# Eight head pairs and the attention gates as seven block products, made behind the first values

## The chip, the cores and the metric

One core of a Trainium2 chip runs the whole layer in one launch. The metric is the time of one execution in device microseconds, taken as the median of several runs. TensorE (PE) multiplies, VectorE (DVE) and ScalarE (ACT) compute on tiles of 128 partitions, GpSimd (POOL) helps, and SyncE (SP) issues most DMAs.

## The reference, cut to what matters

The layer takes 1024 tokens of width 1024. One input projection gives queries, keys and values of 24 heads of width 64, a Fourier input of width 512, and two sigmoid gates of width 1024. The heads stand in three groups of eight, with dilations 1, 4 and 16.

```
proj = x @ w_in                      # 1024 x 7168
q, k, v = 24 heads of 64 each;  u_f = 512 columns
gate_a, gate_f = sigmoid(two slices of 1024 columns)
for each group: banded attention, queries scaled by 1/8, bias by T5 bucket
attn   = softmax over groups of the log-sums, applied to the three outputs
merged = gate_a * (attn @ w_attn_out) + gate_f * (fourier(u_f) @ w_fourier_out)
h = layer_norm(ALPHA * x + merged @ w_out)
h = layer_norm(ALPHA * h + squared_relu_mlp(h))
```

## The kernel before

All large products are split in two float32r parts, high and low: `split` (L62) rounds on ACT (L63) and takes the rest on DVE (L64), and `mm3` (L73) issues three matmuls (L75 to L77) for each pair of 128 x 128 weights and 128 x 512 data.

The activations come transposed, as eight tiles of 128 channels x 1024 tokens. The kernel loads and splits one after the other and keeps the parts `xh`, `xl` in the ring `U` (31 slots of 4 KB a partition) until the last gate is made. While they come in, the values of group 0 are accumulated over the eight tiles in all eight PSUM banks (L113 to L141). Other rings are `wr` (3 raw weights), `w` (10 split weights), `S` (8 half tiles) and `PT` (6 half tiles).

Twelve head pairs follow (L368 to L379). Before each `attention` the pair's queries and keys are made by `project` (L182): two blocks of 128 columns, each of two halves of tokens and eight contraction tiles, so 96 matmuls, straight into `U` tiles in SBUF. Groups 1 and 2 turn the token order as they copy out of PSUM (L194 to L203). `values` (L143) makes all eight value tiles of the next group at once, behind the second pair of a group. `attention` (L222) works in units: scores on PE (L237), bias and running minimum on DVE (L245), exponent on ACT (L248), transposes on PE (L262), copies on DVE and ACT (L270 to L276), products with the values (L291), copies out (L303). At its end ACT issues the small DMAs of the row sums (L322 to L328; four to a pair in groups 0 and 2, sixteen in group 1).

The Fourier branch comes next. In its last loop (L546) each of eight column blocks makes its gate from `xh`, `xl` (`gates`, L338, 48 matmuls) and `combine` (L421) joins the three groups' outputs of one head pair from DRAM, behind blocks 1, 3, 5 and behind the loop. Then the attention output runs over eight column blocks: `gates("wga", d)`, 48 matmuls, and `attn_out` (L583), 24 matmuls, with the gate applied on DVE (L590, L591).

The up-projection of the MLP (L782) already makes pairs of column blocks as seven products of half-sized blocks in place of eight, by Strassen and Winograd's scheme: `weight_blocks` (L711) forms sums of weight blocks (L733 to L739) and splits them, `token_blocks` (L676) sums of token blocks, and each product takes 12 matmuls into a PSUM bank that later products add to.

The instructions of each engine are put in order by a scheduler when the kernel is built: among those whose inputs are ready by its cost model, the one that stands earlier in the program goes first. On the chip each engine takes its instructions in that order and waits at the first that is not ready. Tiles of a ring are handed out as others come free.

Of the kernel before, what the change touches and what calls it, by code (L numbers as in the profile page):

```python
# [11 lines left out]
F32 = mybir.dt.float32  # L12
F32R = mybir.dt.float32r
AF = mybir.ActivationFunctionType
ALU = mybir.AluOpType
# [13 lines left out]
def tile_hybrid_layer(ctx, tc, a, out):  # L29
# [57 lines left out]
    make_identity(nc, ident)  # L87


    xh, xl = [], []  # L90

    def v_cols(g, t):
        if g == 0:
            return slice(64 + 128 * t, 192 + 128 * t)
# [4 lines left out]

    def v_lhs(g, t, k):  # L100
        if g == 0 and t == 7:
            return xeh[:, k, :], xel[:, k, :]
# [6 lines left out]
    V = {0: v_alloc()}  # L109
    xTk = a["xT"].rearrange("(k p) n -> p k n", p=128)  # L110
    accs = [ps(t) for t in BANKS]
    vw = {}
    for k in range(8):  # L113
        x = wr([128, 1024])
        xh.append(U([128, 1024], F32R, "xh"))
        xl.append(U([128, 1024], F32R, "xl"))
        if k == 0:
            w0 = tmp([128, 512]), tmp([128, 512])
            for c in range(2):
                s = slice(512 * c, 512 * c + 512)  # L120
                nc.sync.dma_start(x[:, s], a["xT"][0:128, s])
                nc.sync.dma_start(w0[c], a["wv"][0, 0, :, c])
                split(x[:, s], xh[0][:, s], xl[0][:, s])
                vw[c] = tmp([128, 512], F32R), tmp([128, 512], F32R)
                split(w0[c], *vw[c])
            xeh, xel = U([128, 8, 128], F32R, "xe"), U([128, 8, 128], F32R, "xe")
# [3 lines left out]
            split(xer, xeh, xel)  # L130
        else:
            nc.sync.dma_start(x, a["xT"][128 * k:128 * k + 128])
            split(x, xh[k], xl[k])
            if k % 2 == 0:
                w = weights(a["wv"][0, k // 2], [128, 2, 512])
                for c in range(2):
                    vw[k + c] = w[0][:, c], w[1][:, c]
        for t in range(8):
            mm3(accs[t], *v_lhs(0, t, k), *vw[k], k == 0, k == 7)
    for t in range(8):  # L140
        (nc.vector.tensor_copy if t % 2 else nc.scalar.copy)(V[0][t // 2][:, t % 2], accs[t])  # L141

    def values(g):  # L143
        V[g] = v_alloc()
        w = [weights(a["wv"][g, u], [128, 2, 512]) for u in range(4)]
        for t in range(8):
# [3 lines left out]
            (nc.vector.tensor_copy if t % 2 else nc.scalar.copy)(V[g][t // 2][:, t % 2], p)  # L150


    bd = dram.tile([24, NE], F32, name="bd")
# [16 lines left out]
    def bias_tile(g, hp):  # L170
        n = 128 if g == 2 else 256
        b = tmp([128, 2, 256], name="bias")
        for hh in range(2):
            off = bd.offset + (8 * g + 2 * hp + hh) * NE + E_OFF[g]
            nc.sync.dma_start(b[:, hh, :n], bass.AP(tensor=bd.tensor, offset=off, ap=[[1, 128], [1, n]]))
        return b


    od = dram.tile([3, 4, 128, 1024], F32, name="od")
    sd = dram.tile([3, 4, 4, 1024], F32, name="sd")  # L180

    def project(g, hp):  # L182
        qk = []
        for i in range(2):
# [183 lines left out]
    todo = [(g, hp) for g in range(3) for hp in range(4)]  # L368
    cur = project(0, 0)
    bias_rows()  # L370
    for i, (g, hp) in enumerate(todo):
        bias = bias_tile(g, hp)
        attention(g, hp, *cur, bias)
        if hp == 1 and g < 2:
            values(g + 1)
        if i + 1 < len(todo):
            cur = project(*todo[i + 1])
# [168 lines left out]
    for d in range(8):  # L546
        if d == 1:
            group_weights()
        gate = gates("wgf", d, tmp) if d else gate_f0
        if d == 3:  # L550
            w4n = fourier_weights(1)
        if d % 4 == 0:
            w4, ws = w4n
        dc = slice(128 * (d % 4), 128 * (d % 4) + 128)
        yp = []
        for c0, c1 in CC:
            p = ps("s")[:, :c1 - c0]
# [24 lines left out]

    def attn_out(d, gate):  # L583
# [127 lines left out]
    def weight_blocks(pair, which):  # L711

        (wa, *wb), _ = WR.pop(pair)
        out = WB[pair]

        def put(name, src):
            t = out[name] = wh([128, 2, 512], F32R, "wb")
            split(src, t[:, 0], t[:, 1])

        sum_ = nc.vector.tensor_tensor  # L720
        a11, a12 = wa[:, :512], wa[:, 512:]
        if which != 1:
            put("A11", a11)
            put("A12", a12)
        if which == 0:
            return
        a21, a22 = wb[0][:, :512], wb[0][:, 512:]
        if pair < WHOLE:
            put("A21", a21)
            put("A22", a22)  # L730
            return
        s3 = tmp([128, 512], name="s3")
        sum_(s3, a11, a21, op=ALU.subtract)  # L733
        sum_(a21, a21, a22, op=ALU.add)
        sum_(a11, a21, a11, op=ALU.subtract)
        put("S2", a11)
        put("S1", a21)
        put("S3", s3)
        sum_(a12, a12, a11, op=ALU.subtract)  # L739
        put("S4", a12)  # L740
        put("A22", a22)


    WHOLE, START = 2, 5
# [3 lines left out]
    for hf in range(2):  # L748
        zs = [U([128, 1024], name="z") for _ in range(4)]
        stats = []  # L750
        for c in range(2):
            s = slice(512 * c, 512 * c + 512)
            w = [weights(a["wout"][c, u], [128, 2, 512]) for u in range(4)]
            for t in range(4):
# [12 lines left out]
                else:  # L767
# [376 lines left out]
```

## Time and profile before

| what | value |
|---|---|
| median of three runs | 1634.26 us (1632.04 to 1637.53) |
| profiled execution: time, span | 1630.72 us, 1628.9 us |
| PE busy | 1586.7 us, 97% of the span |
| DVE busy | 932.5 us, 57% |
| ACT busy | 604.0 us, 37% |
| POOL busy | 268.2 us, 16% |
| first projection begins | 52.98 us |
| attention stage | about 77 to 566 us |
| attention output | about 760 to 870 us |

The profile is of one execution. A busy share says how much of the span had an instruction of the engine in flight; consecutive matmuls overlap, so the distance between their starts, not the length of one, is what each costs.

### The profile page before, as it was taken

To read this page: it belongs to the slowest core of one execution; us is meant where nothing else is said; L and a number is where in the kernel's file an instruction comes from. 1 tells how busy PE (TensorE), PEld (TensorE's weight loads), DVE (VectorE), ACT (ScalarE), POOL (GpSimd) and SP (SyncE) were. 2 spreads that over 40 slices of the span, in tenths; PEclk is the share of its full clock that TensorE was granted. 3 is DMA by queue.
4 is the path that set the end of the run, shared out by engine and by line. 5 is a ranking of instruction groups with operands and counts; after the bars stand their busy time and mean duration, and the time that the engine had idled before them with its cause. 6 is when DMAs were issued, how large, how long until landed. Compare 5 with 4: busy or idle time off the path is not lost. (4 is left out here: it accounts for less than half of the span.)

```text
span 1628.9 us, 20580 instructions
## 1 busy us (share of the span) xinstructions
PE 1586.7 (97%) x7780; PEld 1296.0 (80%) x7780; DVE 932.5 (57%) x1541; ACT 604.0 (37%) x1208; POOL 268.2 (16%) x282
## 2 busy tenths in 40 slices
PE   8999999999999999999999999999999989999997
PEld 6779877897777787888888887888888778888885
DVE  4241333313233287554335787567877997878878
ACT  4251344314334454222213346553444433334312
POOL 0000001100000030000000000043333442526414
PEclk9999999999999999999999999999999999999998
DMA  7210211102111252544114442344436754535502
GB/s 225 78 55 21 78 47 53 59 15 71 56 56 44 73 169 76 172 144 143 52 65 140 157 162 106 121 155 145 152 136 240 263 193 150 181 104 168 168 14 91
DMA packets 79117, 187.25 MB, mean 115 GB/s; under 512 B 11512, under 2 KB 15032, under 8 KB 79018
## 3 DMA queue, kind: packets, MB, share of 16 engines
q1 hardware_dynamic: 64234, 151.56, 28.7%
q0 software_dynamic: 6304, 21.07, 3.3%
q10 hardware_dynamic: 8480, 13.31, 2.2%
q8 instruction: 61, 1.00, 0.3%
q14 instruction: 38, 0.31, 0.1%
HBM read 143.05 MB, written 42.86 MB: 114 GB/s over the span
## 5 line engine op out<-in xcount | busy, mean ns | idle before, releaser
L64 DVE TENSOR_TENSOR w<-wr,w 128x1024 fp32r<-128x1024 f32 x83 | 101.4, 1224 | 288.3 <-ACT w L63 288.2
L75 PE MATMUL pmm<-xh,w 128*128 128x512 f32 x640 | 253.1, 395 | 1.0 <-ACT gate L344 1.0
L77 PE MATMUL pmm<-xh,w 128*128 128x512 f32 x640 | 253.3, 396 | 0.0
L76 PE MATMUL pmm<-xl,w 128*128 128x512 f32 x640 | 252.6, 395 | 0.0
L63 ACT CAST w<-wr 128x1024 fp32r<-128x1024 f32 x83 | 87.2, 1051 | 232.1 <-PE pmm L76 184.6
L75 PEld LDWEIGHTS pmm<-xh,w 128*128 128x128 f32 x640 | 120.2, 188 | 29.4 <-issue 1.5
L76 PEld LDWEIGHTS pmm<-xl,w 128*128 128x128 f32 x640 | 120.1, 188 | 29.1 <-issue 1.2
L77 PEld LDWEIGHTS pmm<-xh,w 128*128 128x128 f32 x640 | 120.1, 188 | 28.1 <-issue 0.7
L965 POOL TENSOR_TENSOR U<-wr,U 128x1024 fp32r<-128x1024 f32 x31 | 88.8, 2878 | 135.4 <-ACT U L963 87.7
L866 POOL TENSOR_TENSOR q<-q,q 128x512 f32<-128x512 f32 x14 | 21.9, 1564 | 539.6 <-ACT q L804 429.0
L64 DVE TENSOR_TENSOR wb<-wup,wb 128x512 fp32r<-128x512 f32 x92 | 73.9, 807 | 45.4 <-ACT wb L63 45.2
L63 ACT CAST w<-U 128x1024 fp32r<-128x1024 f32 x49 | 51.2, 1048 | 125.2 <-PE ppt L76 52.9
L248 ACT ACTIVATE prob<-prob,st 128x192 f32<-128x192 f32 (+2 forms) x192 | 83.9, 439 | 30.9 <-DVE st L245 30.6
L63 ACT CAST wb<-wup 128x512 fp32r<-128x512 f32 x92 | 56.4, 623 | 98.7 <-DVE q L806 60.9
L77 PE MATMUL pmm<-tb,wb 128*128 128x512 f32 x224 | 88.9, 397 | 1.3 <-DVE wb L64 1.3
L75 PE MATMUL pmm<-tb,wb 128*128 128x512 f32 x224 | 89.0, 397 | 0.2 <-ACT part L798 0.2
L76 PE MATMUL pmm<-tb,wb 128*128 128x512 f32 x224 | 89.0, 397 | 0.0
L64 DVE TENSOR_TENSOR w<-U,w 128x1024 fp32r<-128x1024 f32 x49 | 81.3, 1660 | 10.2 <-ACT w L63 10.1
L245 DVE CUSTOM_DVE_ANT_0 prob<-ps,bias 128x192 f32<-128x192 f32 (+2 forms) x192 | 55.8, 348 | 44.6 <-PE ps L237 37.5
L277 POOL MEMSET pt<- 64x128 f32 x80 | 16.0, 200 | 379.0 <-PE po L291 350.5
L963 ACT CAST U<-wr 128x1024 fp32r<-128x1024 f32 x49 | 50.6, 1046 | 36.8 <-DMA wr<-qd 16.5
L75 PE MATMUL ps<-w,U 128*128 128x512 f32 x144 | 57.5, 399 | 2.7 <-DVE acc L1019 2.7
(378 smaller groups left out, 3690.7 us busy)
## 6 DMA issues: line engine op xcount, KB each, us to landing
wr<-qd SPq DMA_DIRECT2D x49, 512.0 KB
wup<-in_wup_dram SPq DMA_DIRECT2D x36, 512.0 KB
qd<-q POOLq DMA_DIRECT2D x56, 256.0 KB, 2.4
U<-in_wdn_dram SPq DMA_DIRECT2D x28, 512.0 KB
wr<-in_wqk_dram SPq DMA_DIRECT2D x24, 512.0 KB
qd<-q ACTq DMA_DIRECT2D x42, 256.0 KB
wr<-in_wout_dram SPq DMA_DIRECT2D x16, 512.0 KB
od<-o POOLq DMA_DIRECT2D x12, 512.0 KB, 3.0
```

The costliest lines, as they stand in the source:

```text
L63: nc.scalar.copy(h, src)
L64: nc.vector.tensor_tensor(l, src, h.bitcast(F32), op=ALU.subtract)
L75: nc.tensor.matmul(o, lh, rh, start=first, stop=False, skip_group_check=on)
L76: nc.tensor.matmul(o, lh, rl, start=False, stop=False, skip_group_check=on)
L77: nc.tensor.matmul(o, ll, rh, start=False, stop=last, skip_group_check=on)
L245: nc.vector.tensor_tensor_reduce(out=e, in0=pp[hh][:, step * i:step * i + n], in1=bias[:, hh, bs], scale=-1.0, scalar=3e38, op0=ALU.add, o ...
L248: nc.scalar.activation(e, e, AF.Exp, bias=m, scale=-1.0, accum_out=st[:, 1, hh, b:b + 1])
L277: nc.gpsimd.memset(t[64 - p0:128 - p0, s], 0.0)
L866: pool(s3, q[11], q[21], op=ALU.subtract)
L963: nc.scalar.copy(h_, r)
L965: sub(l_, r, h_.bitcast(F32), op=ALU.subtract)
```

## The change

Eight head pairs (three of group 0, three of group 1, two of group 2) and the eight blocks of the attention output's gate (as four pairs) are made by seven block products each, right behind the first values. Their results go to DRAM through half tiles (`qkd`, `gd`) and are loaded again by `project` and `gate_rows`. The sums of x blocks (`x_sums`) are formed while x comes in, which now comes in the order 0, 4, 1, 5, 2, 6, 3, 7. The values of group 0 go to DRAM too (`vd`) and come back ahead of the first attention. `values` makes a quarter behind each pair of the group before, holding its eight split weights over the four quarters. `combine` moves to blocks 1, 2, 4 and 5. Pairs (0,0), (1,2), (2,1) and (2,3) are projected as before.

```diff
+    def x_sums(k, ra, rb):
+        b11, b12, b21, b22 = ra[:, :512], ra[:, 512:], rb[:, :512], rb[:, 512:]
...
+        sub(t3, b22, b12, op=ALU.subtract)
+        sub(b12, b12, b11, op=ALU.subtract)
+        sub(b11, b22, b12, op=ALU.subtract)
+        sub(b21, b21, b11, op=ALU.subtract)
+        for n, src in (("T1", b12), ("T2", b11), ("T3", t3), ("T4", b21)):
+            split(src, *(v[:, k % 2] for v in XT[n][k // 2]))
-    for k in range(8):
-        x = wr([128, 1024])
+    for j, k in enumerate((0, 4, 1, 5, 2, 6, 3, 7)):
+        x = raw[k] = (wr if k < 4 else wh)([128, 1024], name="x")
...
+        if k >= 4:
+            x_sums(k - 4, raw[k - 4], raw[k])
+    vd = dram.tile([8, 128, 512], F32, name="vd")
     for t in range(8):
-        (nc.vector.tensor_copy if t % 2 else nc.scalar.copy)(V[0][t // 2][:, t % 2], accs[t])
+        v = half([128, 512], name="v")
+        (nc.vector.tensor_copy if t % 2 else nc.scalar.copy)(v, accs[t])
+        nc.scalar.dma_start(vd[t], v)
-    def values(g):
+    def values(g, quarter):
+        if quarter == 0:
+            V[g] = v_alloc()
+            VW[g] = [weights(a["wv"][g, u], [128, 2, 512]) for u in range(4)]
+        w = VW[g]
+        for t in range(2 * quarter, 2 * quarter + 2):
...
+    AHEAD = [(0, 1), (0, 2), (0, 3), (1, 0), (1, 1), (1, 3), (2, 0), (2, 2)]
+    XKEYS = AHEAD + list(range(0, 8, 2))
+    XFIRST = 3
...
+        def product(x, y, b, tag=None):
...
+            for k in range(4):
+                ks = slice(128 * k, 128 * k + 128)
+                mm3(bank[b], w[x][:, 0, ks], w[x][:, 1, ks], *x_block(y, k), bool(tag) and k == 0, k == 3, True)
+        def keep(name, i):
+            part[name] = tmp([128, 512], name="part")
+            nc.scalar.mul(part[name], bank["x"], scales[i])
+        def emit(i, c, b, name=None):
...
+            if name:
+                t = part[name]
+                if gate:
+                    nc.vector.tensor_tensor(t, t, p, op=ALU.add)
...
+                    nc.vector.scalar_tensor_tensor(ov, pv, scales[i], tv, op0=ALU.mult, op1=ALU.add)
+            if gate:
+                nc.scalar.activation(o, p, AF.Sigmoid)
...
+            nc.scalar.dma_start(dst, ov)
...
+    for j in range(len(st)):
+        if j + 1 < len(st):
+            a_blocks(*x_load(j + 1), XW[j + 1], 1 if j + 1 < XFIRST else 2)
+        more = XFIRST <= j + 1 < len(st)
+        st[j]["p6"]()
+        if j:
+            st[j - 1]["p4"]()
+        st[j]["p5"]()
+        if more:
+            st[j + 1]["p1"]()
+        st[j]["p7"]()
+        if j:
+            st[j - 1]["p3"]()
+        if more:
+            st[j + 1]["p2"]()
...
+        if (g, hp) in AHEAD:
+            with tc.issue_after(after):
+                for i in range(2):
+                    qk.append(U([128, 1024], name="qk"))
+                    nc.sync.dma_start(qk[i], qkd[g, hp, i])
+            return qk
...
-        if hp == 1 and g < 2:
-            values(g + 1)
+        if g < 2:
+            values(g + 1, hp)
...
-        if d in (1, 3, 5):
-            combine(d // 2)
-    gate_a0 = gates("wga", 0, tmp)
-    combine(3)
+        if d in (1, 2, 4, 5):
+            combine({1: 0, 2: 1, 4: 2, 5: 3}[d])
...
-        g = gates("wga", d, tmp) if d else gate_a0
+        g = gate_rows(d)
```

`a_blocks` is the former `weight_blocks` with its tiles as arguments; the up-projection calls it unchanged. The first three keys make their products p1 and p2 from the first half of their weights, ahead of the loop, and load both halves again for the rest.

## Rows read from the trace of the kernel before

**Rows 1.** The page's head, its first part and PE's busy tenths in 40 slices.

```profile
span 1628.9 us, 20580 instructions
PE 1586.7 (97%) x7780; PEld 1296.0 (80%) x7780; DVE 932.5 (57%) x1541; ACT 604.0 (37%) x1208; POOL 268.2 (16%) x282
PE   8999999999999999999999999999999989999997
```

**Rows 2.** Windows: stretch, its length, busy time (instructions) by engine, PEclk, DMA share, GB/s.

```profile
0.00:40.00 40.00, 34.78 (x137) 27.68 (x138) 19.84 (x21) 18.63 (x20) 1.10 (x8) 1.00 0.73 227
960.00:1000.00 40.00, 36.51 (x164) 28.71 (x163) 35.00 (x61) 28.00 (x57) 0.00 (x0) 0.98 0.41 135
1058.00:1240.00 182.00, 182.00 (x786) 147.32 (x786) 139.09 (x160) 81.22 (x134) 73.31 (x79) 1.00 0.40 143
1120.00:1160.00 40.00, 40.00 (x174) 32.39 (x173) 31.91 (x38) 17.96 (x31) 15.60 (x18) 1.00 0.43 154
```

**Rows 3.** Waits of PE: tile and line, releaser: total us, times, longest.

```profile
PE pmm L75 <- ACT PT L63: 5.2, 1, 5.2
PE pmm L75 <- ACT gate L344: 1.0, 1, 1.0
```

**Rows 4.** Timeline of PE: start, length, instruction; where the first projection begins.

```profile
52.98 0.40 PE L75 MATMUL pmm<-xh,w 128*128 128x512 f32 x1
```

**Rows 5.** Timeline of DVE: last split of x, first eviction of values, first bias.

```profile
30.91 1.22 DVE L64 TENSOR_TENSOR xl<-wr,xh 128x1024 fp32r<-128x1024 f32 x1 [0.34 <-ACT xh L63]
...
48.99 0.69 DVE L141 COPY v<-pmm 128x512 f32<-128x512 f32 x1 [4.89 <-PE pmm L77]
...
85.44 0.36 DVE L245 CUSTOM_DVE_ANT_0 prob<-ps,bias 128x192 f32<-128x192 f32 x1 [6.79 <-DMA bias<-bd]
```

**Rows 6.** Lines, 0 to 85 us: group, count | busy us, mean ns | idle before.

```profile
L64 DVE TENSOR_TENSOR PT<-PT,PT 128x512 fp32r<-128x512 f32 x2 | 1.4, 691 | 1.6 <-ACT PT L63 1.6
```

**Rows 7.** Lines by form, 1058 to 1240 us: blocks, copies and sums of the up-projection.

```profile
L64 DVE TENSOR_TENSOR wb<-wup,wb 128x512 fp32r<-128x512 f32 x55 | 47.9, 871 | 27.3 <-ACT wb L63 27.2
L63 ACT CAST wb<-wup 128x512 fp32r<-128x512 f32 x55 | 34.2, 622 | 76.9 <-DVE q L806 60.9 <-PE pmm L77 7.9 <-PE ps L77 7.4
L798 ACT COPY part<-pmm 128x512 f32<-128x512 f32 x27 | 15.7, 583 | 15.3 <-PE pmm L77 15.3
L811 DVE TENSOR_TENSOR part<-part,ps 128x512 f32<-128x512 f32 x18 | 12.3, 684 | 13.3 <-ACT part L798 13.3
L733 DVE TENSOR_TENSOR s<-wup,wup 128x512 f32<-128x512 f32 x9 | 6.2, 684 | 0.0
```

**Rows 8.** Line L818, its issues on ACT: ns min/median/max, first and last start.

```profile
L818 ACTq DMA_DIRECT2D qd<-q x42: 326/326/327, 998.3 to 1293.2; - x42
```

**Rows 9.** Timeline of PE over the attention of group 0, pair 0.

```profile
86.61 1.44 PE L237 MATMUL ps<-qk,qk 64*128 64x256 f32 x8
...
91.01 1.09 PE L262 MATMUL ppt<-ident,prob 128*128 128x128 f32 x8 [0.58 <-ACT pt L276]
...
100.11 0.28 PE L315 MATMUL ppt<-ident,st 128*32 128x128 f32 x1
```

**Rows 10.** Timeline of ACT: attentions of groups 0 and 1, pair 0 of each.

```profile
85.85 0.46 ACT L248 ACTIVATE prob<-prob,st 128x192 f32<-128x192 f32 x1 [9.14 <-DVE st L245]
...
100.77 1.57 ACTq L322 DMA_DIRECT2D sd<-ss  x4
...
271.30 0.46 ACT L248 ACTIVATE prob<-prob,st 128x192 f32<-128x192 f32 x1 [1.57 <-DVE st L245]
...
285.60 10.62 ACTq L325 DMA_DIRECT2D sd<-ss  x16
296.32 1.08 ACT L201 ACTIVATE qk<-pmm 128x512 f32<-128x512 f32 x2 [10.75 <-DMA sd<-ss]
```

**Rows 11.** Waits of ACT: tile and line, releaser: total us, times, longest.

```profile
ACT gate L344 <- DVE PT L433: 12.8, 5, 3.9
```

**Rows 12.** Timeline of DVE in the attention output: one gate times its product.

```profile
793.78 0.69 DVE L590 TENSOR_TENSOR gate<-gate,ps 128x512 f32<-128x512 f32 x1 [0.71 <-PE ps L77]
```

More of the change, by code (lines that the diff above doesn't have):

```diff
@@ L125, in tile_hybrid_layer @@
                 split(w0[c], *vw[c])
-            xeh, xel = U([128, 8, 128], F32R, "xe"), U([128, 8, 128], F32R, "xe")
+            xeh, xel = ([half([128, 4, 128], F32R, "xe") for _ in range(2)] for _ in range(2))
             xer = wr([128, 8, 128])
@@ L129, in tile_hybrid_layer @@
             nc.sync.dma_start(xer[:, :, 64:128], xTk[:, :, 0:64])
-            split(xer, xeh, xel)
+            for i in range(2):
+                split(xer[:, 4 * i:4 * i + 4], xeh[i], xel[i])
         else:
@@ L138, in tile_hybrid_layer @@
         for t in range(8):
[L139 removed]
+            mm3(accs[t], *v_lhs(0, t, k), *vw[k], j == 0, j == 7)
+        if k >= 4:
+            x_sums(k - 4, raw[k - 4], raw[k])
+    vd = dram.tile([8, 128, 512], F32, name="vd")
     for t in range(8):
[L141 to L146 removed]
+        v = half([128, 512], name="v")
[7 more added lines that the diff above has]
+        for t in range(2 * quarter, 2 * quarter + 2):
             p = ps("mm")
@@ L150, in values, with a_blocks, put @@
             (nc.vector.tensor_copy if t % 2 else nc.scalar.copy)(V[g][t // 2][:, t % 2], p)
+    VW = {}
+    def a_blocks(wa, wb, out, which=2, whole=False):
+        def put(name, src):
+            t = out[name] = wh([128, 2, 512], F32R, "wb")
+            split(src, t[:, 0], t[:, 1])
+        sum_ = nc.vector.tensor_tensor
+        a11, a12 = wa[:, :512], wa[:, 512:]
+        if which != 1:
+            put("A11", a11)
+            put("A12", a12)
+        if which == 0:
+            return
+        a21, a22 = wb[:, :512], wb[:, 512:]
+        if whole:
+            put("A21", a21)
+            put("A22", a22)
+            return
+        s3 = tmp([128, 512], name="s3")
+        sum_(s3, a11, a21, op=ALU.subtract)
+        sum_(a21, a21, a22, op=ALU.add)
+        sum_(a11, a21, a11, op=ALU.subtract)
+        put("S2", a11)
+        put("S1", a21)
+        put("S3", s3)
+        sum_(a12, a12, a11, op=ALU.subtract)
+        put("S4", a12)
+        put("A22", a22)
@@ new lines, in tile_hybrid_layer, with x_load @@
+    AHEAD = [(0, 1), (0, 2), (0, 3), (1, 0), (1, 1), (1, 3), (2, 0), (2, 2)]
+    XKEYS = AHEAD + list(range(0, 8, 2))
+    XFIRST = 3
+    XW = [{} for _ in XKEYS]
+    def x_load(j, both=True):
+        key = XKEYS[j]
+        src = (a["wga"][key], a["wga"][key + 1]) if isinstance(key, int) else [a["wqk"][key[0], key[1], i] for i in range(2)]
+        r = [wr([128, 1024], name="wx") for _ in range(2 if both else 1)]
+        for t, v in zip(r, src):
+            nc.sync.dma_start(t, v.rearrange("p k c -> p (k c)"))
+        return r
@@ new lines, in tile_hybrid_layer, with x_block, x_steps, turned @@
+    for j in range(XFIRST):
+        a_blocks(x_load(j, False)[0], None, XW[j], 0)
+    def x_block(y, k):
+        if y in XT:
+            return [v[:, k % 2] for v in XT[y][k // 2]]
+        kk, c = k + 4 * (y[1] == "2"), int(y[2]) - 1
+        return [v[kk][:, 512 * c:512 * c + 512] for v in (xh, xl)]
+    qkd = dram.tile([3, 4, 2, 128, 1024], F32, name="qkd")
+    gd = dram.tile([8, 128, 1024], F32, name="gd")
+    def x_steps(key, w):
+        bank, part = {}, {}
+        gate = isinstance(key, int)
+        scales = (1.0, 1.0) if gate else (QK_SCALE, 1.0)
+        g = 0 if gate else key[0]
+        def turned(t, n):
+            return t if g == 0 else t.rearrange("p (r j) -> p r j", r=n)
+        def product(x, y, b, tag=None):
+            if tag:
+                bank[b] = ps(tag)
+            for k in range(4):
[5 more added lines that the diff above has]
+        def emit(i, c, b, name=None):
+            n = (1, 4, 8)[g]
+            o, p = half([128, 512], name="qo"), bank[b]
+            ov = turned(o, n)
+            pv = p if g == 0 else p.rearrange("p (j r) -> p r j", r=n)
+            if name:
+                t = part[name]
+                if gate:
+                    nc.vector.tensor_tensor(t, t, p, op=ALU.add)
+                    p = t
+                else:
+                    tv = t if g == 0 else t.rearrange("p (j r) -> p r j", r=n)
+                    nc.vector.scalar_tensor_tensor(ov, pv, scales[i], tv, op0=ALU.mult, op1=ALU.add)
+            if gate:
+                nc.scalar.activation(o, p, AF.Sigmoid)
+                dst = gd[key + i]
+            else:
+                if not name:
+                    nc.scalar.mul(ov, pv, scales[i])
+                dst = qkd[key[0], key[1], i]
+            m = 512 // n
+            dst = dst[:, 512 * c:512 * c + 512] if g == 0 else turned(dst, n)[:, :, m * c:m * c + m]
+            nc.scalar.dma_start(dst, ov)
+        def p1():
+            product("A11", "B11", "x", "mm")
+            keep("r1", 0)
+        def p2():
+            product("A12", "B21", "y", "pt")
+            emit(0, 0, "y", "r1")
+        def p6():
+            product("S2", "T2", "x")
+            keep("r2", 0)
+        def p5():
+            product("S1", "T1", "z", "s")
+        def p7():
+            product("S3", "T3", "x")
+            keep("r3", 1)
+            emit(1, 1, "z", "r3")
+        def p4():
+            product("A22", "T4", "x")
+            emit(1, 0, "x")
+        def p3():
+            product("S4", "B22", "z")
+            emit(0, 1, "z", "r2")
+        return dict(p1=p1, p2=p2, p3=p3, p4=p4, p5=p5, p6=p6, p7=p7)
@@ new lines, in tile_hybrid_layer @@
+    st = [x_steps(key, w) for key, w in zip(XKEYS, XW)]
+    for j in range(XFIRST):
+        st[j]["p1"]()
+        st[j]["p2"]()
+    a_blocks(*x_load(0), XW[0], 1)
+    for j in range(len(st)):
[13 more added lines that the diff above has]
+            st[j + 1]["p2"]()
@@ L174, in bias_tile, with project @@
             off = bd.offset + (8 * g + 2 * hp + hh) * NE + E_OFF[g]
-            nc.sync.dma_start(b[:, hh, :n], bass.AP(tensor=bd.tensor, offset=off, ap=[[1, 128], [1, n]]))
-        return b
+            last = nc.sync.dma_start(b[:, hh, :n], bass.AP(tensor=bd.tensor, offset=off, ap=[[1, 128], [1, n]]))
+        return b, last.ins
     od = dram.tile([3, 4, 128, 1024], F32, name="od")
     sd = dram.tile([3, 4, 4, 1024], F32, name="sd")
-    def project(g, hp):
+    def project(g, hp, after=None):
         qk = []
+        if (g, hp) in AHEAD:
+            with tc.issue_after(after):
+                for i in range(2):
+                    qk.append(U([128, 1024], name="qk"))
+                    nc.sync.dma_start(qk[i], qkd[g, hp, i])
+            return qk
         for i in range(2):
@@ L370, in tile_hybrid_layer @@
     bias_rows()
+    V[0] = v_alloc()
+    for u in range(4):
+        nc.sync.dma_start(V[0][u], vd[2 * u:2 * u + 2].rearrange("t p c -> p t c"))
     for i, (g, hp) in enumerate(todo):
-        bias = bias_tile(g, hp)
+        bias, mark = bias_tile(g, hp)
         attention(g, hp, *cur, bias)
-        if hp == 1 and g < 2:
-            values(g + 1)
+        if g < 2:
+            values(g + 1, hp)
         if i + 1 < len(todo):
-            cur = project(*todo[i + 1])
+            cur = project(*todo[i + 1], mark)
         if i + 2 == len(todo):
@@ L576, in tile_hybrid_layer, with gate_rows @@
         merged.append(y)
-        if d in (1, 3, 5):
-            combine(d // 2)
-    gate_a0 = gates("wga", 0, tmp)
-    combine(3)
+        if d in (1, 2, 4, 5):
+            combine({1: 0, 2: 1, 4: 2, 5: 3}[d])
+    def gate_rows(d):
+        g = []
+        for c in range(2):
+            g.append(tmp([128, 512], name="gate"))
+            nc.sync.dma_start(g[c], gd[d, :, 512 * c:512 * c + 512])
+        return g
     def attn_out(d, gate):
@@ L713, in weight_blocks @@
         (wa, *wb), _ = WR.pop(pair)
[L714 to L741, printed above, removed]
+        a_blocks(wa, wb[0] if wb else None, WB[pair], which, pair < WHOLE)
     WHOLE, START = 2, 5
```

19 lines of the change are left out of this document (14 added, 5 removed).

## The prediction

> **What bounds the kernel now.** I read the page's head first: PE is busy 1586.7 of 1628.9 us and no slice before the last is below eight tenths, while DVE stands at 57% and ACT at 37% [rows 1]. Then the windows, since an average hides stages. In a stretch of the MLP PE is busy all 40 us with 174 matmuls of 512 columns [rows 2], so one costs 40 / 174 = 0.230 us. The worst inner window, 960 to 1000 us, loses 3.5 us, with DVE busy 35 of 40 [rows 2]. Last the waits of PE: apart from 5.2 us at the start, where nothing has arrived yet, the attention gates' wait is 1.0 us in total [rows 3]. So there is little idle time to win, and the span is nearly the sum of what PE must do. Fewer matmuls count in full unless another engine takes over.
>
> One reading could go wrong here. The timeline gives a matmul a length of 0.40 us [rows 4], and by that length 144 fewer would be worth 57.6 us; by the distance of starts they are worth 33.1. The Trainium skill (Trainium Kernel Development and Optimization, Performance Expectations) calls matmul busy time a bad metric because matmuls are pipelined, and prefers the busy share of weight loads. The windows agree: 174 lengths of 0.40 us do not fit into 40 us one after another. The weight loads' share of the page is 80%.
>
> **The matmuls removed.** A pair of column blocks took 2 x 2 x 8 x 3 = 96 matmuls, and takes 7 x 4 x 3 = 84 now. Eight head pairs and four gate pairs make 12 x 12 = 144 fewer, 144 x 0.230 = 33.1 us. Nothing else of PE's work changes in number: the values are the same matmuls in another place, and the attentions the same.
>
> **The first values.** DVE has to form and split x sums while x arrives: per pair of x tiles four sums and four splits, eight instructions of 128 x 512 at 0.691 us [rows 6], 5.5 us, four times, 22.1 us. In the first 40 us DVE is busy 19.84 [rows 2], so about 20 us are free; its last split of x starts at 30.91 [rows 5], the projection behind the values at 52.98 [rows 4]. Three of the four x_sums stand ahead of the last split: 32.1 + 16.6 = 48.7 us even if none falls into idle time, and PE needs that tile at 52.98 - 24 x 0.230 = 47.5. So the end is nearly covered. In the middle it is tighter: the first x_sums stands ahead of the split of the third tile, and can hold PE there for a microsecond or two. If the cover is gone, all 22.1 us are on the path; none is a gain. I take 2 us. ACT's added casts, 16 x 0.62 = 10 us [rows 7], fit beside its 18.63 [rows 2]. The copies of the values go on to DRAM through ACT's queue at 0.326 us an issue [rows 8], eight of them, beside the first products.
>
> **The block products.** The up-projection shows this scheme at work: from 1058 to 1240 us PE is busy 182.00 of 182 [rows 2]. A pair here has 84 x 0.230 = 19.3 us of PE. DVE does seven splits (0.871 each, slow end), four block sums and three joins (0.684) [rows 7]: 6.1 + 4.8 = 10.9 us. ACT does seven casts at 0.622, three copies at 0.583, one scaled copy of the same size, and four issues at 0.326 [rows 7, 8]: 8.0 us; four sigmoids for a gate pair in place of the one copy add some 2. Weights in and results out are 2.1 MB, 109 GB/s, under half of the 227 that the first 40 us carried [rows 2]. The rings are the next question: with one slot of `w` kept for x, nine remain, and counting live blocks product by product each block is written at least three products (8 us) before it is used. So I take nothing. If that is wrong, the nearest row is the window at 960 us: 3.5 us lost of 40 [rows 2] over 12 x 19.3 = 232 us would be 20 us. A gain beyond the removed matmuls is excluded, for PE was dense before. The start of this part is covered by the first two products of three pairs, 3 x 24 x 0.230 = 16.6 us. Writing turned rows in short runs may lengthen transfers, but a pair's results have eight half tiles to wait in and a hundred microseconds before anyone reads them.
>
> **The attention stage with less to fill it.** Before, 22.1 us of projection followed every attention. Now eight of the first nine boundaries have only a quarter of the values, 48 x 0.230 = 11.0 us. An attention takes PE from 86.61 to 100.4, 13.8 us [rows 9], with one wait of 0.58 us inside: it runs dense almost unaided. ACT needs from 85.85 to 102.34 for it in group 0, 16.5 us, the four issues of row sums included [rows 10], against 13.8 + 11.0 = 24.8 of PE: covered. In group 1 it needs from 271.30 to 296.2, 24.9 us, of which 10.62 are sixteen issues that hold everything behind them [rows 10]. That equals PE's 24.8. Behind (1,1) the projection of (1,2) adds 22.1 us of cover; behind (1,0), (1,2) and (1,3) nothing does, and behind (1,0) the split of the next values' weights (four casts, 4.2 us by twice the 0.622 of the smaller form [rows 7]) competes for the same ACT. I take 4 us in all; the ends are 0 and 3 x 10.62 = 31.9. The first bias tile makes DVE wait 6.79 us [rows 5]; the projection filled it, now the first quarter of values must, and if its weights are late the price is that 6.8. The loads of queries and keys stand in SP's queue behind the bias of the attention before, 25 us ahead of use, and a pair's 1.05 MB takes 4.6 us at 227 GB/s [rows 2]; late, they would cost up to 4.6 each time. The reload of the first values, 2.1 MB or 9.2 us, has the projection of (0,0) before it, 22.1 us.
>
> **The Fourier loop and the attention output.** `combine` now runs in two neighbouring blocks twice and takes the half tiles that the gates want. That conflict exists: ACT's gates wait 12.8 us for `combine`'s sums [rows 11], of which PE felt 1.0 [rows 3]. I take 1 us more, with ends 0 and 12.8. In the attention output a block shrinks to 24 x 0.230 = 5.5 us of PE against four DVE instructions of 0.69 [rows 12], 2.8 us, and 0.52 MB of gates, 95 GB/s. Covered, nothing.
>
> **The sum.** 33.1 - 2 - 0 - 4 - 1 = 26.1 us. The profiled execution took 1630.7 us (its span and 1.8 around it), so 1604.6; the median of the runs shown lies 3.5 us above it, and by the same difference I forecast 1608 us for the median.
>
> **The rivals.** First, DVE sets the first stage: the order in which x arrives makes each x_sums stand in front of a split that PE waits for. For it speaks that DVE's load there doubles; against it the 20 us of idle time. All 22.1 us exposed: 33.1 - 22.1 - 5 = 6, or 1628.
>
> Second, ACT's sixteen issues of group 1 come out at three boundaries: 31.9 in place of 4, a sum of -1.8, or 1636; two of three, 1625. For it speaks that ACT waited 10.75 us behind them [rows 10] where PE still had a projection to do; against it that PE's quarter of values is as long. The Trainium skill (TensorE: Matmul & The Clock Gate, Architectural detail) says that ScalarE's queue is strictly first in, first out; by it nothing ready can pass those issues, and the row with 10.75 us agrees.
>
> Third, the other side: ACT's chain and the fillers of groups 0 and 1 run one after the other, since the order is fixed at build time by a model that may take the issues for cheap. ACT's eight attentions are 4 x 16.5 + 4 x 24.9 = 166 us, the fillers 8 x 11.0 + 22.1 = 110, together 276 against 8 x 13.8 + 110 = 221 on PE: 55 us more, net 33.1 - 3 - 55 = -25, or 1659 us. It decides from about 30 of these 55 us on. Against it: in the trace PE takes projection matmuls inside an attention's gaps, and waits 0.58 us in one [rows 9].
>
> Fourth, everything is hidden, and freeing x earlier takes a little off the window at 960 us: 1597 to 1601.
>
> **How the numbers follow.** The forecast has 0.62 (its own range 1600 to 1616), the first rival 0.13 (1620 to 1631), the second 0.13 (1620 to 1637), the third 0.06 (1640 to 1660), the fourth 0.06. The range is 1598 to 1631. About 0.3% (5 us) is what can be told from no change. Faster by more, below 1629.4: 0.62 + 0.06 + 0.10 + 0.04 = 0.82. Within it: 0.03 + 0.08 = 0.11. Slower: 0.07.
>
> **What would show it.** PE's count falls from 7780 to 7636. Behind the first values a stretch of 230 us should hold 174 matmuls in 40 us with PE's waits near zero; waits there for a split would mean that the rings bind. The first block product should begin near 55 us; at 65 or later the x sums bind. In group 1, waits of PE for exponents or for split value weights of about 10 us would show ACT's issues. The attention output should last about 45 us. The prediction is wrong if PE has idle stretches of more than 10 us in all that were not there before.

## The result and the profile after

The changed kernel takes 1619.55 us (median; 1613.07 to 1620.28) against 1633.15 us before in the same session: a ratio of 0.990, 95% interval 0.988 to 0.992. A second session gave 1619.34 us and 0.991 (0.988 to 0.993). So it is faster by about 1%, 14 to 16 us of the 33.1 us of matmuls that it no longer issues. The forecast of 1608 us was 11.5 us too low; its range held the time.

The profiled execution took 1613.07 us, the shortest of its runs, so the gain by trace is 17.6 us where 26.1 were forecast. First the page: its head, first part and PE's tenths, as in [rows 1].

```profile
span 1611.3 us, 20786 instructions
PE 1560.5 (97%) x7636; PEld 1272.1 (79%) x7636; DVE 1037.8 (64%) x1718; ACT 648.1 (40%) x1299; POOL 267.9 (17%) x282
PE   8999999999999999899999999999999989999997
```

PE's count is 7636, 144 fewer. DVE gained 105 us and ACT 44, and PE's share stayed at 97%: neither became the bound. The page cannot say where the other 15 us went. For that I cut both traces at the same events and held each stage against what its matmuls are worth at 0.230 us.

| stage, from event to event | before | after | due after | over |
|---|---|---|---|---|
| start to first block product (before: first projection) | 53.0 | 53.9 | 53.0 | +0.9 |
| 1008 matmuls of the block products | | 235.4 | 231.7 | +3.7 |
| first scores to last row sums (768 matmuls left) | 486.5 | 314.3 | 309.9 | +4.4 |
| first merge of the Fourier loop to first product with `w_out` out (384 left) | 239.1 | 158.4 | 150.8 | +7.6 |
| all other stages together | | | | -1.0 |

The sum is 15.6, which leaves 17.5 of 33.1. The block products in windows, with the columns of [rows 2]:

```profile
0.00:40.00 40.00, 33.70 (x133) 26.49 (x134) 30.55 (x44) 22.13 (x31) 0.70 (x6) 1.00 0.63 197
40.00:80.00 40.00, 39.35 (x169) 31.25 (x167) 21.32 (x33) 13.35 (x23) 0.00 (x0) 1.00 0.45 154
80.00:120.00 40.00, 39.52 (x170) 31.81 (x171) 25.71 (x39) 16.31 (x30) 0.00 (x0) 1.00 0.40 132
120.00:160.00 40.00, 40.00 (x174) 32.43 (x173) 20.86 (x29) 13.71 (x24) 0.00 (x0) 1.00 0.33 105
...
748.00:751.00 3.00, 0.17 (x1) 0.17 (x2) 1.38 (x2) 0.69 (x2) 0.00 (x0) 1.00 0.81 223
751.00:754.00 3.00, 3.00 (x9) 2.31 (x10) 1.38 (x2) 1.05 (x3) 0.00 (x0) 0.59 0.91 334
754.00:757.00 3.00, 3.00 (x13) 2.40 (x12) 2.89 (x8) 2.28 (x5) 0.00 (x0) 0.84 0.03 10
```

DVE goes from 19.84 to 30.55 us busy in the first 40 and still costs PE only four matmuls there. From 120 us on, 174 matmuls fit into 40 us, as many as in the stretch of the up-projection [rows 2]. The two windows before it hold 169 and 170: nine matmuls, 2 us, with waits of 0.5 and 0.6 us for a weight split. Behind the second stands a late load: SP waited 17.4 us for a split to free a slot of `wr` before it could issue it.

The last three rows show the one place where PE stood still. Its waits, to compare with [rows 3] (tile and line, releaser: total us, times, longest):

```profile
PE pmm L75 <- ACT PT L63: 5.3, 1, 5.3
PE pmm L75 <- ACT gate L537: 5.0, 2, 3.0
...
PE ps L75 <- DVE mg L767: 2.1, 1, 2.1
...
PE ppt L455 <- ACT prob L441: 1.7, 1, 1.7
```

The gates' wait was 1.0 us in total; now it is 5.0, and `ps` at the head of the attention output (L767 is the merge that holds the bank) adds 2.1. From 748 to 751 us PE issues one matmul. In the next 3 us the granted clock is 0.59, near the lower of its two levels (1.2 of 2.4 GHz), then 0.84; at the full clock these two windows would have taken 3 x 0.41 + 3 x 0.16 = 1.7 us less. So 5.0 - 1.0 + 2.1 + 1.7 = 7.8, against 7.6 in the table.

What the gate waits for stands on ACT's timeline, to be read beside [rows 11] (start, length, instruction, idle before and releaser):

```profile
745.82 0.62 ACT L63 CAST ath<-PT 128x512 fp32r<-128x512 f32 x1 [4.10 <-DVE PT L631]
750.18 1.33 ACT L537 ACTIVATE gate<-pmm 128x512 f32<-128x512 f32 x2 [3.74 <-DVE PT L629]
```

ACT stands idle for 3.74 us with the matmuls of the gate done, since the half tile it writes to is one of the six in `PT`, and `combine`'s sum at L629 still uses it. PE needs the gate's PSUM bank for the next block, and stops 3.01 us. That sum in turn waits for its operands:

```profile
ACT gate L537 <- DVE PT L629: 11.1, 4, 3.8
...
DVE PT L629 <- DMA PT<-ad: 23.6, 15, 2.8
```

In the second session's trace the same waits return (3.77, 1.43 and 2.15 us; first scores to last row sums 315.5 us, the loop's stretch 161.1), and its clock behind the first is lower still:

```profile
754.06:757.00 2.94, 2.94 (x7) 2.36 (x8) 1.07 (x2) 0.60 (x1) 0.00 (x0) 0.50 0.90 335
757.00:760.00 3.00, 3.00 (x9) 2.33 (x9) 2.32 (x8) 2.31 (x5) 0.00 (x0) 0.58 0.08 33
```

That execution took 1619.12 us. Of the 6 us between the two, 1.2 lie in the attentions, 2.8 between them and the loop's stretch, 2.7 in that and 1.0 in the MLP (the stages ahead were 1.6 shorter), and the mean clock is 0.988 against 0.993.

### The profile page after: what moved, and what is told of

Read it like the earlier page. It is cut to its first block, busy times and chain, and to the rows that moved or that the text cites. A ratio compares the mean times of both kernels' runs of the same rounds, so it can differ in the third digit from the quotient of the medians.

```text
span 1611.3 us, 20786 instructions
## 1 busy us (share of the span) xinstructions
PE 1560.5 (97%) x7636; PEld 1272.1 (79%) x7636; DVE 1037.8 (64%) x1718; ACT 648.1 (40%) x1299; POOL 267.9 (17%) x282
## 5 line engine op out<-in xcount | busy, mean ns | idle before, releaser
L64 DVE TENSOR_TENSOR w<-wr,w 128x1024 fp32r<-128x1024 f32 x59 | 71.9, 1222 | 87.9 <-ACT w L63 75.6
L75 PE MATMUL pmm<-xh,w 128*128 128x512 f32 x256 | 102.4, 400 | 5.9 <-ACT gate L537 5.0
L63 ACT CAST w<-wr 128x1024 fp32r<-128x1024 f32 x59 | 62.0, 1050 | 105.3 <-PE pmm L76 68.4
L77 PE MATMUL pmm<-xh,w 128*128 128x512 f32 x256 | 102.4, 401 | 0.0
L76 PE MATMUL pmm<-xl,w 128*128 128x512 f32 x256 | 101.9, 398 | 0.0
L64 DVE TENSOR_TENSOR wb<-wx,wb 128x512 fp32r<-128x512 f32 x72 | 48.8, 689 | 65.3 <-ACT wb L63 65.3
L63 ACT CAST wb<-wx 128x512 fp32r<-128x512 f32 x72 | 43.8, 620 | 103.2 <-PE pmm L77 60.8
L75 PEld LDWEIGHTS pmm<-xh,w 128*128 128x128 f32 x256 | 48.4, 189 | 17.8 <-ACT gate L537 5.9
L75 PE MATMUL pmm<-w,xh 128*128 128x512 f32 x146 | 60.8, 419 | 1.0 <-ACT w L63 1.0
```

Source lines behind the costliest of these rows:

```text
L75: nc.tensor.matmul(o, lh, rh, start=first, stop=False, skip_group_check=on)
L76: nc.tensor.matmul(o, lh, rl, start=False, stop=False, skip_group_check=on)
L77: nc.tensor.matmul(o, ll, rh, start=False, stop=last, skip_group_check=on)
```

## The experiments

Theory: the loss sits in the `PT` half tiles that `combine` and the loop's gates share, and in ACT's row-sum issues in the attentions. Rivals: quartering the values breaks PE's stream; the gate part earns nothing for another reason; the positions of `combine` matter, not its tiles. All kernels are the changed kernel with the edit shown (cut to the lines that matter), each timed against the kernel before; "the stretch" is the one from the first merge to the first output product, that is, the first product with `w_out`; "the attentions" run from first scores to last row sums.

**The loop's gates in a raw weight slot instead of half tiles.**

```diff
+    def gates_wr(name, d):
+        w = weights(a[name][d], [128, 8, 128])
+        t = wr([128, 2, 512], name="gate")
...
-        gate = gates("wgf", d, tmp) if d else gate_f0
+        gate = gates_wr("wgf", d) if d else gate_f0
```

> One part changed in the new kernel: the Fourier loop's gates are written to a slot of the raw-weight ring and no longer to the ring of half tiles that the sums of the three groups use. Theory (the gates wait for half tiles held by those sums, because the sums now stand in neighbouring blocks; the stretch from the first merge to the first output product went from 239.1 to 158.4 us where 150.8 was due): PE's waits for the gate (5.0 us) and for the merged rows (2.1 us) go, the stretch falls to about 151 to 153 us, the ratio to before falls from 0.990 to about 0.985. Rival (the stretch is long because the attention output has no gate products left to cover DVE): the stretch stays at 157 to 159 us, the ratio at 0.990.

Measured: 0.997 (0.996 to 0.998), 1626.87 us; slower than the change. The waits on gates are gone, and a larger one stands in their place (PE's timeline):

```profile
757.67 0.58 PE L75 MATMUL ps<-pth,w 128*128 128x258 f32 x1 [17.89 <-ACT w L63]
```

The second half of the Fourier weights wants all three `wr` slots, and the gates held them. The stretch is 172.9 us. So the waits on gates go when the gates leave the half tiles, as the theory has it, but this run cannot price them: an experiment that moves a tile has to ask who else uses the ring it goes to.

**The head pairs alone.** The gates are made as before, and `combine` is back at its old places.

```diff
-    XKEYS = AHEAD + list(range(0, 8, 2))
+    XKEYS = AHEAD
...
-        g = gate_rows(d)
+        g = gates("wga", d, tmp) if d else gate_a0
```

> Only the eight head pairs are made ahead; the four gate pairs, the places of the sums of the three groups and the gates of the attention output are as in the kernel before. Products saved: 8 x 12 x 0.230 = 22.1 us in place of 33.1. Theory (the 7.6 us lost between the first merge and the first output product belong to the gate part): that stretch is 239 us as before, the profiled span about 1611 to 1614 us, the ratio 0.988 to 0.991, the same as with the gates ahead. Rival (the losses belong to the attention stage and the block products): the time rises by most of the 11 us not saved, ratio 0.995 to 0.997.

Measured: 0.989 (0.987 to 0.991), 1614.66 us. With 48 more matmuls (11.0 us) it is no slower than the whole change; the stretch is 239.7 us as before (239.1) and the attentions 313.3 us.

**The gates alone.** No head pair ahead, values whole behind the second pair.

```diff
-    AHEAD = [(0, 1), (0, 2), (0, 3), (1, 0), (1, 1), (1, 3), (2, 0), (2, 2)]
+    AHEAD = []
```

> Only the four gate pairs are made ahead; all twelve head pairs are projected as in the kernel before and the values are made in one piece; the places of the sums of the three groups are those of the change. Products saved: 4 x 12 x 0.230 = 11.0 us. Theory (the gate part gives back what it saves, 7.6 us between first merge and first output product, and a start of 1 to 3 us): the attention stage lasts 486 us as before, ratio 0.997 to 1.000. Rival (the gate part pays by itself): ratio 0.993 to 0.995.

Measured: 1.000 (0.998 to 1.002), 1632.11 us. The stretch is 159.4 us with PE waits of 3.21, 1.44 and 2.16. So the two halves add up: the head pairs earn all of the gain. Of the gates' 11.0 us of saved matmuls 8.6 (159.4 - 150.8) are given back in the stretch, whether or not head pairs are made ahead. The remaining 2.4 go too, by the trace: the first scores come 79.4 us later for 77.2 us of block products, and the attentions take 0.8 us more.

**The values whole again.** All four quarters behind the second pair, as in the kernel before.

```diff
-        if g < 2:
-            values(g + 1, hp)
+        if hp == 1 and g < 2:
+            for quarter in range(4):
+                values(g + 1, quarter)
```

> The values of the next group are made in one piece behind the second pair of a group, as before the change; everything else as in the new kernel. Theory A (cutting them into quarters breaks them into 28 short runs between attention work, where a matmul takes 0.259 us in place of 0.246; that is 5 us): the runs fall to some 10, the stretch from the first scores to the last row sums falls from 314.3 to 309 to 311 us, ratio 0.986 to 0.988. Rival B (without a quarter behind each pair PE has nothing to do while ACT works at its 16 to 25 us of an attention): PE's idle time there rises by 10 us or more, ratio 0.995 or above.

Measured: 1.001 (0.999 to 1.003), 1634.56 us: the whole gain is lost. Profiled: 1640.88 us, near the top of its runs. Theory A was not tested, since PE's value matmuls still come in 28 separate runs, though two of these now hold 120 and 123 matmuls. The attentions take 331.4 us instead of 314.3. PE's waits there, and then three windows around the last attention of group 1 and the first of group 2 (columns as in [rows 2]):

```profile
PE ppt L455 <- ACT prob L441: 5.3, 3, 2.1
...
PE ppt L455 <- ACT pt L463: 3.1, 1, 3.1
```

```profile
540.00:560.00 20.00, 18.14 (x106) 13.13 (x107) 7.69 (x41) 10.64 (x42) 1.79 (x9) 0.91 0.19 65
560.00:580.00 20.00, 15.46 (x107) 11.09 (x105) 6.31 (x37) 7.22 (x37) 0.53 (x1) 0.89 0.13 41
580.00:600.00 20.00, 18.52 (x108) 14.61 (x109) 6.78 (x27) 9.20 (x27) 0.63 (x2) 0.77 0.38 113
```

The same stretch of time in the changed kernel, which has the projection of (2,1) in one piece there:

```profile
540.00:560.00 20.00, 18.25 (x117) 14.58 (x113) 10.00 (x40) 8.28 (x35) 0.53 (x1) 1.00 0.34 113
560.00:580.00 20.00, 19.62 (x110) 15.40 (x107) 7.95 (x11) 6.48 (x9) 0.64 (x2) 1.00 0.49 166
580.00:600.00 20.00, 19.67 (x139) 15.38 (x138) 8.50 (x57) 11.58 (x51) 0.53 (x1) 1.00 0.15 48
```

Idle time grew by 5 us, and the three windows (20 x (0.09 + 0.11 + 0.23) = 8.6 us) with one more at 0.91 from 440 us (1.8) lost 10.4 us to the clock: together 15 of the 17. So waits of 1.4 to 3.1 us, which the quarters of values had filled, went with a loss to the clock twice as large as the idle time. Another 8.0 us lie between the attentions and the loop (79.1 us instead of 71.1, at a mean granted clock of 0.89 instead of 0.98). The median is 6 us below this execution; how much of the loss to the clock every execution has is not shown.

**The sixteen row-sum issues of group 1 through POOL**, with the change, and with the head pairs alone.

```diff
-                    nc.scalar.dma_start(dst.rearrange("(b h r n) -> r b h n", b=2, h=2, r=4)[r],
+                    nc.gpsimd.dma_start(dst.rearrange("(b h r n) -> r b h n", b=2, h=2, r=4)[r],
```

> The sixteen small DMAs of row sums in each pair of group 1 are issued by POOL and not by ACT, which frees 10.6 us of ACT behind each attention of group 1. Theory (in group 1 ACT's issues equal PE's quarter of values and cost PE nearly nothing; of the 4.4 us lost in the attention stage they are at most the one wait of 1.7 us): the ratio stays within 0.001 of 0.990. Rival (ACT's issues set the pace of group 1): 3 to 10 us less in the attention stage, ratio 0.984 to 0.988.

> Only the eight head pairs ahead, with the small DMAs of group 1 issued by POOL. If the parts add up: 1614.7 less 1 to 2 us, ratio 0.987 to 0.988; against this stands that ACT's issues cost nothing: 0.989.

Measured: 0.988 (0.986 to 0.990) and 0.988 (0.986 to 0.990). The attentions take 313.2 us instead of 314.3 and 312.4 instead of 313.3; the wait of 1.7 us for `prob` (0.9 us with the head pairs alone) is gone. Neither ratio can be told from that of the kernel without the edit. By these two stages ACT's issues cost about 1 us, but in other executions the clock falls at that wait. The first trace of the change and its second one, behind the wait (1.7 and 1.4 us):

```profile
554.00:557.00 3.00, 3.00 (x16) 2.41 (x15) 0.69 (x1) 3.00 (x17) 0.00 (x0) 1.00 0.03 5
```

```profile
551.00:554.00 3.00, 3.00 (x12) 2.26 (x11) 0.08 (x1) 3.00 (x17) 0.00 (x0) 0.55 0.02 5
```

Five traces have the whole change, the values in quarters and these issues on ACT. In two the clock holds there and the attentions take 314.3 and 314.4 us; in three it falls and they take 315.5, 315.5 and 316.6. In the four with POOL's issues they take 313.0 to 313.5. So ACT's issues cost 1 us of the change where the clock holds, and 2 to 3 us where it falls.

**`combine`'s operands out of the half tiles.** First for head pairs 0 to 2 into slots of `U`; then the same, with `combine` one block earlier, the attention output in PSUM banks of its own and POOL's issues.

```diff
-                o, w = tmp([128, 512]), tmp([128, 512])
+                if hp < 3:
+                    ow = U([128, 2, 512], name="ow")
+                    o, w = ow[:, 0], ow[:, 1]
+                else:
+                    o, w = tmp([128, 512]), tmp([128, 512])
```

> One part changed in the new kernel: the sums of the three groups of the first three head pairs load their rows into slots of the ring U; those of the last pair stay in the half tiles. Theory (the gates of the Fourier loop wait because these sums hold the half tiles, and the clock that falls behind PE's 3.0 us wait makes it dearer): the wait near 750 us goes and with it the low clock there (0.59 in the three microseconds behind it), the one near 797 us stays; from first merge to first output product 154 us in place of 158.4, and no runs at a mean clock of 0.988; ratio 0.985 to 0.988. Rival (the loads of the sums and the gate weights are late for another reason, such as the DMA queue): the wait stays, ratio 0.990.

> As the last one, with the sums placed behind blocks 1, 2, 3 and 4, the attention output's products in the three banks that the gates' products have left free, and the sixteen small DMAs of group 1 issued by POOL. Theory: all three waits between first merge and first output product (3.0, 2.0, 2.1 us) go, that stretch is 151 to 152 us, and the attention stage 313 us; the profiled span is about 1601 to 1604 us and the ratio 0.982 to 0.985, faster than the new kernel. Rival (the fourth sum's half tiles only move the wait to an earlier block, and DVE is late at the change of stages): the stretch stays above 155 us, ratio 0.987 or more.

Measured: 0.990 (0.988 to 0.992) and 0.989 (0.987 to 0.991). The first wait went and the other grew. For the first kernel and the second:

```profile
PE pmm L75 <- ACT gate L537: 5.8, 1, 5.8
```

```profile
PE pmm L75 <- ACT gate L537: 8.9, 1, 8.9
```

They end at 798 and 791 us, where head pair 3 still takes half tiles; the stretch is 162.8 and 162.1 us. Moving three of four merely moved the wait to the fourth. The last wait, 2.14 us for the bank, is gone in the second kernel, so that one was the bank.

**All four out of the half tiles.** Head pair 3 takes slots of `w`. First with the free banks and POOL's issues, at the change's positions; then with all four in `U` and one block earlier; then the tiles alone.

```diff
-                o, w = tmp([128, 512]), tmp([128, 512])
+                ow = (U if hp < 3 else wh)([128, 2, 512], name="ow")
+                o, w = ow[:, 0], ow[:, 1]
...
-            p = ps("s")
+            p = ps("mm")
```

> The sums of the three groups load no rows into half tiles any more: those of the first three head pairs use slots of the ring U, those of the last pair slots of the split-weight ring; places as in the change (blocks 1, 2, 4, 5). Also the attention output's products go to the three banks the gates have left, and the small DMAs of group 1 are issued by POOL. Theory (the gates of the loop wait for half tiles that the sums hold; where the first three pairs moved out, only the wait behind the last pair stayed, at 5.8 and 8.9 us): no wait for a gate over 1 us is left, first merge to first output product 151 to 153 us in place of 158.4, profiled span 1601 to 1606 us, ratio 0.981 to 0.985. Rival (the wait follows the loads of the last sums or DVE's load, whichever ring holds them): a wait of 3 us or more stays in that stretch, ratio 0.987 to 0.990.

> As the last, with the sums behind blocks 1 to 4 and all in slots of U. Theory: no wait for a gate over 1 us either, 151 to 154 us, ratio 0.981 to 0.985. Rival (the ring U is full by then, with x, the tables' products, the merged rows and the attention outputs in it, and the merged rows wait in place of the gates): a wait of 3 us or more for merged rows, ratio 0.987 or more.

> Of the three edits of the kernel at 0.9814 only the slots of the sums (ring U for three pairs, the split-weight ring for the last); banks and row sums as in the change. Theory (the slots carry nearly all of it): the two waits for a gate go, the one of 2.1 us for the merged rows stays, first merge to first output product 153 to 155 us, ratio 0.983 to 0.986. Rival (banks and row sums carry it): ratio 0.988 or more.

> The changed kernel as it is, on the chip of the run beside it. Theory: ratio 0.988 to 0.992, three waits of 2 to 3 us between first merge and first output product. If the gate waits are noise of one execution, they are absent here.

| kernel | ratio to before | median us | stretch us |
|---|---|---|---|
| all three edits | 0.981 (0.979 to 0.983) | 1602.57 | 149.4 |
| all in `U`, one block earlier | 0.984 (0.982 to 0.986) | 1606.56 | 149.7 |
| the tiles alone | 0.984 (0.982 to 0.986) | 1609.25 | 153.6 |
| the change again, in the session of the row above | 0.991 (0.988 to 0.993) | 1619.34 | 161.1 |

The tiles alone take 7.5 us off the stretch (4.8 against the first trace of the change) and 10 us off the median, with no wait on a gate left; of what remains there, 2.7 us is the wait for the bank. With the banks too, the stretch is dense (149.17 of 149.40 us):

```profile
698.00:847.40 149.40, 149.17 (x691) 122.75 (x690) 108.97 (x182) 45.92 (x67) 1.54 (x3) 1.00 0.62 176
```

against the changed kernel's

```profile
698.90:857.30 158.40, 151.27 (x691) 123.90 (x690) 110.79 (x182) 46.26 (x67) 1.54 (x3) 0.99 0.53 167
```

So the tiles are the cause of the gates' waits, and the version with all three edits beats both kernels. It earns 29 to 30 us of the 33.1. What banks, POOL and the positions of `combine` add is not separated by the times, since the intervals of the three kernels touch. By the stretch, the free banks add 4 us (153.6 to 149.4; POOL's issues lie in the attentions) and the positions nothing. But the kernel with the earlier positions (and all four pairs in `U`) is 4.9 us longer ahead of the stretch, between the attentions and it. There it has the same longest wait, 2.2 us, and a lower clock. First the kernel with all three edits, then that one:

```profile
625.60:698.00 72.40, 66.01 (x456) 56.91 (x455) 49.34 (x89) 34.10 (x78) 15.92 (x20) 0.98 0.45 142
```

```profile
625.30:702.60 77.30, 70.34 (x456) 60.34 (x455) 50.03 (x89) 34.03 (x78) 15.97 (x20) 0.91 0.42 133
```

Whether the positions bring this about is not shown. Some 3.5 us of the best kernel's profiled time lie in the MLP up to its first sum, which no edit touched (332.5 us, where the changed kernel has 336.0 and the others 334.1 to 338.4). The longer waits there are the same, 1.3 to 1.9 us each, and the clock behind them differs by 1.7 us; the changed kernel and the best one in the same place:

```profile
980.00:984.00 4.00, 3.30 (x8) 2.65 (x9) 1.85 (x4) 1.44 (x3) 0.00 (x0) 0.57 0.99 363
```

```profile
970.00:974.00 4.00, 3.45 (x15) 2.83 (x16) 1.69 (x3) 2.10 (x4) 0.00 (x0) 1.00 0.99 365
```

The rest no run explains.

## Why the prediction was right, and where its sizes were off

The direction, the range and the mechanism held: PE is the bound, fewer matmuls count at 0.230 us each, and some of the steps give part of it back. The sizes of these steps held less well. Step by step:

- **The matmuls removed**, 33.1 us: 144 fewer, and windows of 174 in 40 us. Right.
- **The first values**, 2 us: 0.9. DVE's added sums fit into its idle time; the first rival is out.
- **The block products**, nothing: 3.7 us. It is not the ring of split weights that I weighed: the windows after 120 us are dense. About 2 us lie in the first two windows, at the two waits for splits, and for the second the raw weights' ring `wr` held the load back; no experiment was made on it. The rest is the price itself. A window also counts the matmuls that its two ends cut; the starts stand 0.232 us apart in both traces, which makes 1008 matmuls some 2 us longer than 231.7. At that price the removed matmuls are worth 33.4 us, and the attentions and the Fourier loop gave back 1.5 and 0.8 us more than the table says.
- **The attentions**, 4 us: 4.4, by another cause. I priced ACT's issues behind the attentions of group 1. They do take their 10 us, and what stands behind waits as in [rows 10]:

```profile
432.88 10.66 ACTq L518 DMA_DIRECT2D sd<-ss  x16
443.64 0.59 ACT L175 COPY v<-pmm 128x512 f32<-128x512 f32 x1 [10.79 <-DMA sd<-ss]
...
540.01 11.06 ACTq L518 DMA_DIRECT2D sd<-ss  x16
551.12 0.40 ACT L441 ACTIVATE prob<-prob,st 128x128 f32<-128x128 f32 x1 [11.14 <-DVE st L438]
```

  but PE has the quarter of values beside them, and taking them off ACT gained 1 us there, 2 to 3 where the clock falls. The larger part is the filler itself: the projections that filled PE's gaps are gone, so the values fill them now, in 28 unbroken runs of matmuls where there were 7, and their 384 matmuls take 99.3 us by the distance of starts instead of 94.2. Where a run begins, its first matmul (PE's timeline; the run begins at 337.56) stands 0.46 us before the next:

```profile
336.75 0.88 PE L484 MATMUL po<-pt,v 128*64 128x128 f32 x12
337.56 0.62 PE L77 MATMUL pmm<-w,xl 128*128 128x512 f32 x1
338.02 0.40 PE L75 MATMUL pmm<-w,xh 128*128 128x512 f32 x1
338.25 0.40 PE L76 MATMUL pmm<-w,xh 128*128 128x512 f32 x1
```

  The mean of these first distances is 0.44 us; behind them both traces have a median of 0.24. So each run that begins costs some 0.2 us more, as the traces show; no kernel here has the quarters in fewer runs to test it. Of the 4.4 us, the values make 5.1 and the attentions' own matmuls 2.1, the wait of 1.7 with them, while the projections that are left came out 2.7 below what was due. I had the amount right by accident.
- **The Fourier loop**, 1 us with ends 0 and 12.8: 7.6 us. This is the term that was mis-sized and most of the miss. I saw the conflict and its price on ACT [rows 11], and took from [rows 3] that PE feels a twelfth of it. But that 1.0 belonged to a loop with `combine` two blocks apart; in the changed loop the gate was late by 3.0 and 2.0 us, and the bank's wait and the fall of the clock, which I had not priced, added 2.1 and 1.7. That the half tiles are the cause is shown; that the neighbouring blocks make it worse than before is only argued, since no run has the old positions together with the gates made ahead. And 7.6 is the least of it: five traces keep this loop as it is, and their stretches are 158.4 to 163.1 us, 7.6 to 12.3 above what was due.
- **The attention output**, nothing: its 2.1 us wait lies at its start and is counted above. Its products took 44.7 us, forecast at about 45.

Of the rivals the first and the second did not come; the fourth would have needed every cost hidden. The third, which was to make it slower, did not come by the order of the build. With the values bunched behind the second pairs a part of it shows: PE waits for ACT's exponents and copies, 5 us of idle time and 10 of clock in the attentions, far from the 55 us of that rival, but enough that the gain is gone. The sign that I had named for a wrong prediction, more than 10 us of added idle time, came close: PE's idle time rose from 42.2 to 50.8 us.

The median came out 6.5 us above the profiled execution, not 3.5. The profiled one was the shortest, and the two traces of the same kernel differ by small waits and by what the clock loses behind them.

## What to carry to other kernels

Work that is taken off the bounding engine is only won if the slots that the rest shares do not turn it into a wait: ask for each ring, at the place where operations move together, how many live tiles both users want, and price the conflict by the engine that holds the slot, not by what the bound felt when there was slack. Filler work between latency-bound stages can be worth more than its own time: here the gaps that it had covered cost PE 5 us of idle time and 10 us of clock. When an experiment cures one wait and the total stays, look for the same resource's next user before dropping the theory.

## What the runs showed of the hardware

- One short wait in an otherwise dense PE stream can cost more than half as much again in clock, and does not always. In the two traces of the change, a wait of 3.0 us was followed by two windows of 3 us at 0.59 and 0.84 (1.7 us lost), and one of 3.8 us by 2.9 us at 0.50 and 6 us at 0.79 (2.9 x 0.50 + 6 x 0.21 = 2.7 us lost). At a wait of 1.4 to 1.7 us near 550 us the clock held in two traces and fell in three, and between the attentions and the loop two kernels with the same longest wait of 2.2 us ran at 0.98 and 0.91.
- The weight loads of the values of groups 1 and 2, whose columns are strided, take 321 ns where the same form with dense columns takes 188. Their matmuls stand 0.24 us apart within a run, instead of 0.23, and the first of a run 0.44 us before its second. Weight loads (PEld) of the changed kernel, up to 52 us (values of group 0) and from 313 to 630 us (groups 1 and 2):

```profile
L76 PEld LDWEIGHTS pmm<-w,xh 128*128 128x128 f32 x18 | 3.4, 188 | 0.9 <-DVE w L64 0.2
...
L76 PEld LDWEIGHTS pmm<-w,xh 128*128 128x128 f32 x128 | 41.1, 321 | 0.7 <-issue 0.7
```
